# The fourth weight sum of a Strassen quad, moved from VectorE to an accumulating DMA

## The chip, the cores and the metric

The kernel runs on one core of a Trainium2 chip. The metric is the device time of one execution in microseconds (us); lower is better. The core has a matrix engine (TensorE, PE in the profile, with its weight loads as PEld), VectorE (DVE), ScalarE (ACT), GpSimd (POOL) and SyncE (SP), which mostly issues DMAs. All engines run their own instruction queues in order, and wait for each other through semaphores.

## The reference

One decoder layer on 256 tokens with model width 2048, all in float32: a first SwiGLU block (FFN, width 5632), then a mixer that joins sliding-window attention with a gated linear recurrence (HGRN2), a second SwiGLU block, gated per-layer input embeddings and a final RMSNorm.

```
def swiglu(h, w_gate, w_up, w_down):
    return (jax.nn.silu(h @ w_gate) * (h @ w_up)) @ w_down
...
    h = rmsnorm(x, ffn1_norm[l])
    x = x + 0.5 * swiglu(h, ffn1_w_gate[l], ffn1_w_up[l], ffn1_w_down[l])
    ...
    h = rmsnorm(x, ffn2_norm[l])
    x = x + 0.5 * swiglu(h, ffn2_w_gate[l], ffn2_w_up[l], ffn2_w_down[l])
```

The change lies in the two products `h @ w_gate` and `h @ w_up` of both FFNs.

## The kernel before, in words

**Weights.** All weights pass through the class `Weights` in one fixed order, as tiles of 128 x 1024 floats (512 KB). `load` issues a DMA from SP into a `raw` buffer (8 of them), three tiles ahead. `prep` makes two tiles of each: ACT casts `raw` to `whi` (line 117, `fp32r`), and DVE subtracts, `wlo = raw - whi` (line 118). There are 5 buffers of each. `next` is called by the code that multiplies, and keeps `prep` four tiles ahead of it. A product of float32 quality is made of three matmuls: activation high part by `whi`, activation low part by `whi`, activation high part by `wlo`.

**The FFN groups.** The width 5632 is cut into 11 column blocks of 512, worked in slices of two or three blocks, each followed by its part of the down-projection. In a block, `strassen_group` computes gate and up together. The contraction of 2048 is cut into four quarters, which go by the pattern S, P, S, P. In a P quarter the four weight tiles ("plain tiles") are used as they are, 12 matmuls each. In an S quarter ("quad") the four tiles are one 2 x 2 block matrix: b11 and b21 from gate, b22 and b12 from up. It is multiplied by seven products, Strassen's way, instead of eight; these are roles 0 to 6, six matmuls each. Roles 0, 1 and 2 use b11, b21 and b22 as loaded. The other roles use four sums that are made in place in the raw buffers:

```
b22 = b12 + b22        # used by role 4
b12 = b12 + b11        # used by role 5
b11 = b11 + b22        # used by role 3
b21 = b21 + b11        # used by role 6
```

So roles 3 to 6 each use a sum. All four are DVE instructions of line 101, the three of role 3's `prep` and the one of role 6's. The first FFN has ten such groups (its first column block is done plainly), the second eleven: 21 groups, 42 quads.

**Order.** The program is put in order by a scheduler, which gives each engine a static list: instructions go by priority once their inputs are expected. Loads and `prep` are in a block of high priority. Evictions of PSUM (lines 402 to 418), SiLU (468), the activations' scaling and transposes come between them. A raw buffer is free for the next load when its last reader has finished.

Of the kernel before, what the change touches and what calls it, by code (L numbers as in the profile page):

```python
# [15 lines left out]
ALU = mybir.AluOpType  # L16
# [15 lines left out]
class Weights:  # L32
# [61 lines left out]
    def prep(self, parts=1):  # L94
        nc = self.nc
        i = self.done
        self.done += 1
        while self.loaded < min(i + 1 + (LEAD if i > 12 else 0), len(self.order)):
            self.load(parts)
        key = self.order[i]  # L100
        add = lambda out, a, b: nc.vector.tensor_tensor(out, a, b, op=ALU.add)  # L101
        with self.tc.high_priority(offset=PRIO if i > 12 else 0):
            role = key[-1] if key[0] == "S" else 0
            raws = [self.raws.get(i - role + k) for k in range(4)]
            src = raws[(0, 1, 2, 0, 2, 3, 1)[role]]
            if role == 3:
                b11, b21, b22, b12 = raws
                add(b22, b12, b22)
                add(b12, b11, b12)
                add(b11, b11, b22)  # L110
            elif role == 6:
                add(raws[1], raws[1], raws[0])
            hi, lo = self.tile("whi", i, 5), self.tile("wlo", i, 5)
            n = 1024 // parts
            for p in range(parts):
                c = slice(p * n, (p + 1) * n)
                nc.scalar.copy(hi[:, c], src[:, c])  # L117
                nc.vector.tensor_tensor(lo[:, c], src[:, c], hi[:, c].bitcast(F32), op=ALU.subtract)  # L118
        if key[0] != "S":
            del self.raws[i]  # L120
        elif role == 6:
            for k in range(4):
                del self.raws[i - 6 + k]
        self.ready[i] = (hi, lo)
# [944 lines left out]
```

## Time and profile before

| | |
|---|---|
| median of 3 runs | 2217.03 us (2215.2 to 2217.91) |
| profiled execution | 2218.1 us; span 2216.0 us |
| granted TensorE clock | 0.995 |
| HBM read | 415.03 MB, 188 GB/s over the span |
| DMA queue of SP | 56.1% of 16 engines' span |
| DMA queue of ACT | 0.2% |
| DMAs issued by POOL | none |

The span runs from the first to the last instruction of the profiled execution. In a row of the time order stand the start, the time it took (several merged instructions have their count behind an x), the engine, the source line, the operation, and output and inputs by name; in brackets the engine's idle time before it and what ended it. A row of waits reads: engine, line, what it waited for, us in total, times, longest. `ps` are the PSUM banks of a Strassen group, `as` the activations of an S quarter, `ap` those of a P quarter.

### The profile page before, as it was taken

Reading aid. Unit: us, or ns where it says so; the run is one execution under the profiler, and the core shown is the slowest. Engines: PE = TensorE matmul, PEld = TensorE weight load, DVE = VectorE, ACT = ScalarE, POOL = GpSimd, SP = SyncE. Lnnn points to the kernel's source line nnn. Section 1 sums busy time; section 2 is a strip of 40 time slices with the busy share of each in tenths; the row PEclk is TensorE's granted clock in tenths of the full one; section 3 lists DMA queues with packets and bytes.
Section 4 is the critical chain, followed back from the end, with each engine's and each line's share of the span. In section 5 each row is a group of like instructions: output and inputs, shape, how many; then the busy total and the mean of one; then the engine's idle time right before and its main releaser. Section 6 shows DMA issues by size and latency. Waiting matters only on the chain.

```text
span 2216.0 us, 27978 instructions
## 1 busy us (share of the span) xinstructions
PE 2182.4 (98%) x10400; PEld 1795.3 (81%) x10400; DVE 1666.3 (75%) x1954; ACT 1168.4 (53%) x1482; POOL 12.7 (1%) x26
## 2 busy tenths in 40 slices
PE   8999999999999999999999999999999999999998
PEld 7778888888888888877888888787888888888887
DVE  6987979789796566776455555898897979789654
ACT  7644645455455444556444445565554545545554
POOL 0000000000000000000000000000000000000000
PEclk9999999999999999999999999999999999999999
DMA  8455556646466554544666665456555556646662
GB/s 305 166 204 171 201 180 227 210 171 228 155 245 185 182 166 151 158 146 148 191 190 191 189 190 180 152 193 217 185 217 176 191 189 219 212 177 221 201 195 87
DMA packets 118072, 418.97 MB, mean 189 GB/s; under 512 B 13744, under 2 KB 14128, under 8 KB 117936
## 3 DMA queue, kind: packets, MB, share of 16 engines
q1 hardware_dynamic: 117072, 415.83, 56.1%
q8 instruction: 82, 1.34, 0.2%
q10 hardware_dynamic: 864, 1.35, 0.2%
q14 instruction: 54, 0.44, 0.1%
HBM read 415.03 MB, written 2.10 MB: 188 GB/s over the span
## 4 chain that ended last, share of the span: by engine, by line
PE 94%; DVE 3%; DMA 1%; ACT 1%; issue 1%; POOL 0%; SPq 0%; ACTq 0%; POOLq 0%; DVEq 0%
PE ps L399 38%; PE pa L290 16%; PE pa L291 16%; PE pa L296 16%; PE pb L311 3%; PE pb L313 1%; DVE wlo L118 1%; PE tp L333 1%; PE lv L808 1%; DMA raw<-in_ffn_gate 1%; ACT whi L117 1%; DVE raw L101 1%; DMA x<-in_x 0%; PE tx L506 0%; PE sc L726 0%
## 5 line engine op out<-in xcount | busy, mean ns | idle before, releaser
L118 DVE TENSOR_TENSOR wlo<-raw,whi 128x1024 fp32r<-128x1024 f32 (+1 forms) x907 | 1079.4, 1219 | 446.1 <-ACT whi L117 440.9
L117 ACT CAST whi<-raw 128x1024 fp32r<-128x1024 f32 (+1 forms) x907 | 930.5, 1051 | 888.6 <-PE pa L291 468.1
L399 PE MATMUL ps<-whi,ap 128*128 128x512 f32 x1344 | 337.2, 389 | 3.2 <-ACT whi L117 3.2
L399 PE MATMUL ps<-whi,as 128*128 128x512 f32 x1176 | 318.8, 393 | 4.3 <-DVE ff L464 2.1
L399 PEld LDWEIGHTS ps<-whi,ap 128*128 128x128 f32 x1344 | 251.6, 188 | 57.5 <-ACT whi L117 4.5
L291 PE MATMUL pa<-whi,act 128*128 128x512 f32 x704 | 275.2, 392 | 3.9 <-DVE act L335 3.9
L290 PE MATMUL pa<-whi,act 128*128 128x512 f32 x704 | 277.3, 395 | 0.6 <-ACT act L334 0.6
L399 PEld LDWEIGHTS ps<-whi,as 128*128 128x128 f32 x1176 | 220.9, 189 | 55.8 <-ACT whi L117 3.0
L101 DVE TENSOR_TENSOR raw<-raw,raw 128x1024 f32<-128x1024 f32 x168 | 205.4, 1223 | 4.2
L290 PE MATMUL pa<-whi,hTmx 128*128 128x512 f32 x480 | 192.1, 400 | 0.0
L296 PE MATMUL pa<-wlo,act 128*128 128x512 f32 x704 | 190.2, 392 | 0.0
L291 PE MATMUL pa<-whi,hTmx 128*128 128x512 f32 x480 | 187.4, 391 | 0.0
L399 PE MATMUL ps<-wlo,ap 128*128 128x512 f32 x672 | 183.5, 390 | 2.5 <-DVE wlo L118 2.5
L399 PE MATMUL ps<-wlo,as 128*128 128x512 f32 x588 | 182.9, 392 | 0.0
L291 PEld LDWEIGHTS pa<-whi,act 128*128 128x128 f32 x704 | 132.9, 189 | 31.3 <-DVE act L335 4.6
L290 PEld LDWEIGHTS pa<-whi,act 128*128 128x128 f32 x704 | 132.8, 189 | 27.6 <-ACT act L334 0.9
L296 PEld LDWEIGHTS pa<-wlo,act 128*128 128x128 f32 x704 | 132.1, 189 | 27.3
L399 PEld LDWEIGHTS ps<-wlo,ap 128*128 128x128 f32 x672 | 126.1, 188 | 29.9 <-DVE wlo L118 3.8
L399 PEld LDWEIGHTS ps<-wlo,as 128*128 128x128 f32 x588 | 110.5, 189 | 24.4 <-DVE wlo L118 1.7
L296 PE MATMUL pa<-wlo,hTmx 128*128 128x512 f32 x480 | 128.4, 389 | 0.0
L290 PEld LDWEIGHTS pa<-whi,hTmx 128*128 128x128 f32 x480 | 90.1, 188 | 21.4 <-issue 2.5
L296 PEld LDWEIGHTS pa<-wlo,hTmx 128*128 128x128 f32 x480 | 90.1, 188 | 18.9
(238 smaller groups left out, 1994.2 us busy)
## 6 DMA issues: line engine op xcount, KB each, us to landing
raw<-in_ffn_up SPq DMA_DIRECT2D x176, 512.0 KB, 5.1
raw<-in_ffn_down SPq DMA_DIRECT2D x176, 512.0 KB, 4.7
raw<-in_ffn_gate SPq DMA_DIRECT2D x175, 512.0 KB, 4.7
raw<-in_w_ga SPq DMA_DIRECT2D x32, 512.0 KB, 3.5
raw<-in_w_gb SPq DMA_DIRECT2D x32, 512.0 KB, 3.5
raw<-in_w_out SPq DMA_DIRECT2D x32, 512.0 KB, 3.5
raw<-in_ple_gate SPq DMA_DIRECT2D x32, 512.0 KB, 3.5
raw<-in_w_i SPq DMA_DIRECT2D x16, 512.0 KB, 3.5
```

Of the source, the lines that this page charges most:

```text
L101: add = lambda out, a, b: nc.vector.tensor_tensor(out, a, b, op=ALU.add)
L117: nc.scalar.copy(hi[:, c], src[:, c])
L118: nc.vector.tensor_tensor(lo[:, c], src[:, c], hi[:, c].bitcast(F32), op=ALU.subtract)
L290: nc.tensor.matmul(ps[t], ks[:, 0, tok], hi[:, c], start=(j == 0 and c == 0), stop=False)
L291: nc.tensor.matmul(ps[t], ks[:, 1, tok], hi[:, c], start=False, stop=False)
L296: nc.tensor.matmul(ps[t], ks[:, 0, tok], lo[:, c], start=False, stop=(last and c == 1))
L311: nc.tensor.matmul(ps, hi[:, c], mov(c), start=(first and c == 0), stop=False)
L313: nc.tensor.matmul(ps[:, 0:S], lo[:, c], mov(c)[:, 0], start=False, stop=False)
L333: nc.tensor.transpose(pt[:, c, t * P:(t + 1) * P], srcs[t][:, i * P:(i + 1) * P], ident)
L399: nc.tensor.matmul(bank(i), stat, mov, start=done[i] == 1, stop=done[i] == todo)
L808: nc.tensor.matmul(ps[a * 64:a * 64 + 64, i], k[:, c], q[:, c], start=True, stop=True)
```

## The change

The add of role 6 is taken out. At the end of role 3's sums, three roles earlier in the program, GpSimd issues a DMA that reads b11 and adds it into b21, both in SBUF.

```
             if role == 3:
                 b11, b21, b22, b12 = raws
                 add(b22, b12, b22)
                 add(b12, b11, b12)
                 add(b11, b11, b22)
-            elif role == 6:
-                add(raws[1], raws[1], raws[0])
+                nc.gpsimd.dma_start(b21, b11, accum_op=ALU.add)
```

Role 6's cast and subtract read b21 as before.

More of the change, by code (lines that the diff above doesn't have):

```diff
@@ L110, in prep @@
                 add(b11, b11, b22)
-            elif role == 6:
-                add(raws[1], raws[1], raws[0])
+                nc.gpsimd.dma_start(b21, b11, accum_op=ALU.add)
             hi, lo = self.tile("whi", i, 5), self.tile("wlo", i, 5)
```

## Prediction

> **What bounds the kernel now.** I read the busy times first, then what TensorE (PE) waited for, then the order of time around one Strassen quad.
>
> ```profile
> PE 2182.4 (98%) x10400; PEld 1795.3 (81%) x10400; DVE 1666.3 (75%) x1954; ACT 1168.4 (53%) x1482; POOL 12.7 (1%) x26
> ...
> L118 DVE TENSOR_TENSOR wlo<-raw,whi 128x1024 fp32r<-128x1024 f32 (+1 forms) x907 | 1079.4, 1219 | 446.1 <-ACT whi L117 440.9
> L117 ACT CAST whi<-raw 128x1024 fp32r<-128x1024 f32 (+1 forms) x907 | 930.5, 1051 | 888.6 <-PE pa L291 468.1
> ...
> L101 DVE TENSOR_TENSOR raw<-raw,raw 128x1024 f32<-128x1024 f32 x168 | 205.4, 1223 | 4.2
> ```
>
> PE is busy 98% of the span, so only 2216.0 - 2182.4 = 33.6 us are idle: whatever is taken from VectorE (DVE), no more than that can come back. The four sums of a quad are line 101: 168 adds, so 42 quads, 1.22 us each. The change takes one of each four away: 42 x 1.22 = 51 us of DVE. Does PE wait for them? The waits of PE and ScalarE (ACT):
>
> ```profile
> PE ps L399 <- ACT whi L117: 3.8, 4, 2.6
> PE ps L399 <- DVE wlo L118: 2.5, 3, 1.3
> PE ps L399 <- DVE ff L464: 2.1, 1, 2.1
> PE pa L291 <- DVE act L335: 3.9, 2, 2.8
> ...
> ACT whi L117 <- DVE raw L101: 105.3, 31, 6.6
> ```
>
> ACT waits 105 us for the sums, but PE waits only 3.8 + 2.5 us in the Strassen groups for a whi or wlo tile. The sums are on ACT's path and almost nowhere on PE's. The order of time around one quad, the second of a slice, shows why:
>
> ```profile
> 346.72 5.00 DVE L101 TENSOR_TENSOR raw<-raw,raw 128x1024 f32<-128x1024 f32 x4
> 350.52 1.07 PE L399 MATMUL ps<-whi,as 128*128 128x512 f32 x4
> 350.57 3.91 ACT L117 CAST whi<-raw 128x1024 fp32r<-128x1024 f32 x4 [5.15 <-DVE raw L101]
> 351.66 8.04 DVE L118 TENSOR_TENSOR wlo<-raw,whi 128x1024 fp32r<-128x1024 f32 x7
> 352.92 1.46 SPq L92 DMA_DIRECT2D raw<-in_ffn_gate  x2
> 358.68 1.07 PE L399 MATMUL ps<-whi,as 128*128 128x512 f32 x4
> 359.58 0.61 PE L399 MATMUL ps<-wlo,as 128*128 128x512 f32 x2
> 359.78 1.06 ACT L117 CAST whi<-raw 128x1024 fp32r<-128x1024 f32 x1 [0.30 <-PE ps L399]
> ```
>
> The scheduler already issues the fourth sum directly behind the third. The four adds start at 346.72 and take 5.00; the last needs 1.26 of that, so the third ends at T = 350.46. At T + 0.11 ACT starts the casts of roles 3, 4, 5 and 6. PE begins role 0 at 350.52, role 6 at 358.68, and its wlo matmuls at 359.58.
>
> **What is removed.** After T, DVE's next work is the subtract of role 3, which needs ACT's cast: T + 0.11 + 1.05 = T + 1.16. Before, the fourth add occupied DVE until T + 1.26. So the 1.22 us mostly turn into a wait for that cast; DVE gains 0.1 us per quad where it has nothing else to put there, and up to 1.2 us where an eviction or a scaling is queued. I take the gain as 0. Its upper bound: the PE waits that the shown rows put down to ACT's whi and DVE's wlo, ff and act reach 2.6, 1.3, 2.1 and 2.8 us at the longest, and one add less shortens an episode by at most 1.2 us; four episodes make 5 us. One of them is FFN2's first group:
>
> ```profile
> 1399.97 1.19 PE L399 MATMUL ps<-whi,ap 128*128 128x512 f32 x4 [2.62 <-ACT whi L117]
> 1402.46 1.22 PE L399 MATMUL ps<-wlo,ap 128*128 128x512 f32 x2 [1.30 <-DVE wlo L118]
> ```
>
> **What is added.** Per quad one DMA, issued from GpSimd's queue (POOL), that reads b11 and b21 and writes b21. Its trigger waits for the third add. The one new wait is ACT's cast of role 6, which waits for the landing. Call L the time from T until that cast may start. Before, ACT came to it at T + 2.97 (three casts of about 0.98 behind T + 0.11). From then on ACT stands still until T + L; behind it in ACT's order are the casts of the next plain tiles and the evictions; DVE's subtract of role 6 and all behind it move to T + L + 1.1, where they stood at T + 4.6. DVE is thus later than before once L exceeds about 3.5.
>
> PE has a reserve. Cast (1.05), hand-over and subtract (1.22) take 2.4 us together, and PE wants wlo of role 6 at 359.58, so in this quad L may be 359.58 - 350.46 - 2.4 = 6.7 us before PE waits. The same for the third and fourth quad of the slice, and for the tightest quads elsewhere:
>
> ```profile
> 370.59 1.21 DVE L101 TENSOR_TENSOR raw<-raw,raw 128x1024 f32<-128x1024 f32 x1
> 379.99 0.61 PE L399 MATMUL ps<-wlo,as 128*128 128x512 f32 x2
> 389.12 5.01 DVE L101 TENSOR_TENSOR raw<-raw,raw 128x1024 f32<-128x1024 f32 x4
> 400.42 0.62 PE L399 MATMUL ps<-wlo,as 128*128 128x512 f32 x2
> ...
> 81.43 5.00 DVE L101 TENSOR_TENSOR raw<-raw,raw 128x1024 f32<-128x1024 f32 x4
> 91.54 0.62 PE L399 MATMUL ps<-wlo,as 128*128 128x512 f32 x2
> ...
> 1419.63 5.00 DVE L101 TENSOR_TENSOR raw<-raw,raw 128x1024 f32<-128x1024 f32 x4
> 1430.64 0.62 PE L399 MATMUL ps<-wlo,as 128*128 128x512 f32 x2
> 1502.18 5.00 DVE L101 TENSOR_TENSOR raw<-raw,raw 128x1024 f32<-128x1024 f32 x4
> 1512.68 0.62 PE L399 MATMUL ps<-wlo,as 128*128 128x512 f32 x2
> ```
>
> Third quad: T = 371.80, reserve 379.99 - 371.80 - 2.4 = 5.8. Fourth: T = 392.87, reserve 5.15. FFN1's second quad: T = 85.17, reserve 4.0. Second and last quad of FFN2's first slice: T = 1423.37 and 1505.92, reserves 4.9 and 4.4; the five quads from the one to the other lie between 4.4 and 5.2, mean 4.8.
>
> The first quad of a slice is different: PE takes the first plain tile after role 4, before roles 5 and 6.
>
> ```profile
> 326.10 5.01 DVE L101 TENSOR_TENSOR raw<-raw,raw 128x1024 f32<-128x1024 f32 x4
> 329.95 4.85 ACT L117 CAST whi<-raw 128x1024 fp32r<-128x1024 f32 x5 [5.15 <-DVE raw L101]
> 336.76 1.98 PE L399 MATMUL ps<-whi,ap 128*128 128x512 f32 x8
> ```
>
> T = 329.85. That plain tile is ACT's fifth cast, behind role 6. To be ready at 336.76 it must start by 335.6, so L may be 335.6 - 329.85 - 0.98 = 4.8.
>
> Eight slices (all but the first of each FFN) repeat this pattern of four. A stall of PE adds to the end one for one, since PE has no idle time left to absorb it. So the cost in us is: 8 x (L - 4.8) + 8 x (L - 5.15) + 8 x (L - 5.8) + 9 x (L - 6.7) + 5 x (L - 4.8) + (L - 4.0), each term only where positive (the nine include one quad of FFN1's first slice; in its other two, and in FFN2's first quad, PE already waits for other things).
>
> **The size of L.** No accumulating or SBUF-to-SBUF DMA is in the trace. The nearest rows are plain loads:
>
> ```profile
> DMA to landing us min/median/max: 3.3/4.1/9.7
> ...
> L92 SPq DMA_DIRECT2D raw<-in_ffn_gate x177: 327/328/732, 1.2 to 2006.0; - x177
> ...
> DMA packets 118072, 418.97 MB, mean 189 GB/s; under 512 B 13744, under 2 KB 14128, under 8 KB 117936
> ...
> raw<-in_w_ga SPq DMA_DIRECT2D x32, 512.0 KB, 3.5
> ...
> wide<-in_masks SPq DMA_DIRECT2D x1, 256.0 KB, 2.6
> ```
>
> Landings count from the issue; 256 KB land in 2.6 us, 512 KB in 3.5, so 0.9 us per 256 KB on a fixed 1.7. The sum must read two tiles of 512 KB; counting both, 1.7 + 4 x 0.9 = 5.3. With the wake-up (0.1) and an issue at least as dear as SP's (0.33 us) L = 5.8. Ends: 3.4 (the fastest plain landing plus the wake-up, as if the second read were free) and 9.7 (the slowest landing). I stay at 5.8, as twice the bytes of the nearest undisturbed row.
>
> The Trainium skill, "DMA: Bandwidth & Descriptors" (Anatomy of one DMA — SWDGE (gpsimd) path), fits a GpSimd DMA as 2.0 us + bytes / 436e3, which makes 3.2 us for 512 KB; the fastest landing of 3.3 agrees for a plain load. "Collectives: The Full Stack" (The bandwidth ceiling) says that a reducing DMA runs at about half the rate because it reads two sources on one ring, not because the add costs anything; by both pages an estimate is 2.0 + 2 x 1.2 = 4.4 us, and the sum would be about 0.4 us, no change. No trace here shows such a DMA.
>
> **The sum** at L = 5.8: 8 x 1.0 + 8 x 0.65 + 0 + 0 + 5 x 1.0 + 1.8 = 20 us, removed adds 0. Against the profiled execution (span 2216.0, 2218.1 in all, 1.1 above the median of the runs, 2217.0) this gives 2238, and 2237 on the median's scale. At L = 7 the formula gives 59 us, at 8 it gives 98.
>
> **Other queues.** POOL is passed by 42 triggers; what else it holds near them is small, such as the next row, which DVE releases 9 us after the third add of that quad (1393.78 + 1.22): cost 0.
>
> ```profile
> 1393.78 1.22 DVE L101 TENSOR_TENSOR raw<-raw,raw 128x1024 f32<-128x1024 f32 x1
> ...
> 1404.24 0.70 POOL L262 TENSOR_TENSOR rstdf<-rstdf,nhalf 128x2 f32<-128x2 f32 x1 [31.62 <-DVE rstdf L261]
> ```
>
> SP loads wait for raw buffers, and b11's now also waits for the DMA's read: T + 5.8 where it was T + 2.4. Loads of the next quad went out from 352.92; they can take the buffers of roles 4 and 5 first, one subtract (1.2 us) later each, and land by 354.1 + 4.1 = 358.2, before the cast that needs the first, 359.78. So 0; without that cover the 1.2 us would show once per quad. The DMA engines move 42 x 1 MB more reads, a tenth of the 419 MB; loads that cross it may land a microsecond later, which the same reserve hides.
>
> **The rivals.** (1) No change: the landing is shorter, because undisturbed it grows by only (3.3 - 2.6) = 0.7 per 256 KB: 1.9 + 2.8 + 0.1 = 4.8. The cost is 0.8 us: 2218. For it: little traffic right after T, since SP's next loads start 2.4 us later. Against: POOL's issue is then free. The two pages of the Trainium skill named above make this rival the likelier one. (2) Faster: the second read costs nothing, L = 3.4, below every reserve, and DVE's freed slots shorten the busy stretches: up to 5 us, 2212. It decides below L = 4.0. Against it: most stalls there start from ACT or from PSUM evictions as much as from the add. (3) Much slower: the add passes through the engines as three passes per byte (read, read, write), 1.7 + 6 x 0.9 + 0.4 = 7.5; the formula gives 78 us: 2295. Nothing in the trace speaks for or against.
>
> **How the numbers follow.** The forecast (L from 5.05 to 7.0) has 0.45, rival 1 0.28, rival 2 0.10, rival 3 with all beyond 7 0.17. A measurement can tell 0.2% (4.4 us) from no change: the cost passes 4.4 at L = 5.05. Hence faster 0.10, same 0.28, slower 0.62. The range runs from 2213, rival 2's side, to 2300; what is left out is below 0.2. Slower cases alone: 2222 to 2300.
>
> **What would show it.** Right: 126 adds in line 101; a cast of role 6 that waits 2 to 4 us for a raw<-raw DMA in most quads; PE waits on whi and wlo in the first and fourth quads of the slices, about 20 us more, none in the second. Wrong: PE's waits unchanged (L below 4.8); or all quads with waits of several us (L beyond 7); or ACT's order changed so that plain tiles are cast before role 6, which would lift the first quads' reserve and take 8 us off.

## The result, and the profile after

| | before | after |
|---|---|---|
| median of 4 runs each | 2217.47 us | 2240.55 us (2239.13 to 2242.07) |
| ratio after / before | | 1.0108 (95% interval 1.0096 to 1.012) |
| profiled execution, span | 2218.1, 2216.0 us | 2241.86, 2240.1 us |
| granted clock | 0.995 | 0.993 |

The kernel is 23 us slower; 2237 had been predicted. The busy times and groups of the profile page after:

```profile
PE 2190.5 (98%) x10400; PEld 1793.6 (80%) x10400; DVE 1617.3 (72%) x1912; ACT 1160.8 (52%) x1482; POOL 49.1 (2%) x68
...
q0 software_dynamic: 6048, 22.02, 5.2%
...
PE 58%; issue 18%; DVE 13%; DMA 4%; ACT 2%; POOL 0%; ACTq 0%; POOLq 0%; SPq 0%; DVEq 0%
...
L117 DVE TENSOR_TENSOR wlo<-raw,whi 128x1024 fp32r<-128x1024 f32 (+1 forms) x907 | 1082.8, 1219 | 519.5 <-ACT whi L116 508.8
...
L101 DVE TENSOR_TENSOR raw<-raw,raw 128x1024 f32<-128x1024 f32 x126 | 154.1, 1223 | 3.4
...
raw<-raw POOLq DMA_DIRECT2D x42, 512.0 KB, 4.5
```

The change did what it says. There are 126 adds where there were 168, DVE's busy time fell from 1666.3 to 1617.3 us, and GpSimd issues 42 DMAs that land 4.5 us after their issue. But in front of its subtracts DVE now idles 519.5 us instead of 446.1: 73 us more, where it was spared 49. The chain of work that ended last, before 94% PE, is now only 58% PE and runs through DVE (13%) and the new DMA (4%) as well; its 18% of "issue" is time for which the profile shows no wait. Of the 24.1 us between the two spans, 16.0 are more idle time of PE (2240.1 - 2190.5 = 49.6, before 33.6). The other 8.1 are longer busy time of PE on the same 10400 matmuls; the profile models where a matmul ends, so part of it can be short waits. Line numbers after the edit are one lower than before.

The waits after (engine, line, what it waited for: us in total, times, longest):

```profile
ACT whi L116 <- DVE raw L101: 156.5, 37, 6.7
...
ACT whi L116 <- DMA raw<-raw: 68.3, 33, 3.8
...
PE ps L398 <- ACT whi L116: 9.8, 11, 3.5
...
PE tp L332 <- DVE ff L474: 3.4, 4, 0.9
...
PE tp L332 <- DVE ff L472: 3.1, 4, 0.8
```

ACT waits 2.1 us at a time for the new DMA (68.3 / 33). PE's own waits for `whi` rose from 3.8 to 9.8 us. The last two rows, transposes (`tp`) that wait for the gated activations (`ff`) at the end of a slice, did not stand among PE's waits before.

Where the time went, from the first loads of three weights in the three traces (`w_i` is first loaded as FFN1 ends, `ple_gate` as FFN2 ends; `w_out`'s last load is the mixer's end). The rows are those of the raw tiles' loads, before and then after; the two times are the first and the last issue:

```profile
L92 SPq DMA_DIRECT2D raw<-in_w_out x32: 327/328/328, 1269.9 to 1355.3; - x32
L92 SPq DMA_DIRECT2D raw<-in_ple_gate x32: 327/328/328, 2076.2 to 2171.6; - x32
L92 SPq DMA_DIRECT2D raw<-in_w_i x16: 327/328/328, 703.4 to 954.9; - x16
```

```profile
L92 SPq DMA_DIRECT2D raw<-in_w_out x32: 327/328/328, 1281.8 to 1367.1; - x32
L92 SPq DMA_DIRECT2D raw<-in_ple_gate x32: 327/328/328, 2100.2 to 2195.6; - x32
L92 SPq DMA_DIRECT2D raw<-in_w_i x16: 327/328/328, 715.1 to 966.5; - x16
```

FFN1 takes 715.1 - 703.4 = 11.7 us more. The mixer takes (1367.1 - 715.1) - (1355.3 - 703.4) = 0.1, FFN2 (2100.2 - 1367.1) - (2076.2 - 1355.3) = 12.2, the rest 0.1. The loss lies in the FFNs alone. Matching the same-numbered matmuls of both traces cuts it further: FFN1's first slice +3.5, its other four +8.2; FFN2's first slice +2.2, its other four +10.

### The profile page after: what moved, and what is told of

The parts are those of the page before. It is cut to its first block, busy times and chain, and to the rows that moved or that the text cites. A ratio compares the mean times of both kernels' runs of the same rounds, so it can differ in the third digit from the quotient of the medians.

```text
span 2240.1 us, 28073 instructions
## 1 busy us (share of the span) xinstructions
PE 2190.5 (98%) x10400; PEld 1793.6 (80%) x10400; DVE 1617.3 (72%) x1912; ACT 1160.8 (52%) x1482; POOL 49.1 (2%) x68
## 3 DMA queue, kind: packets, MB, share of 16 engines
q0 software_dynamic: 6048, 22.02, 5.2%
## 4 chain that ended last, share of the span: by engine, by line
PE 58%; issue 18%; DVE 13%; DMA 4%; ACT 2%; POOL 0%; ACTq 0%; POOLq 0%; SPq 0%; DVEq 0%
PE ps L398 19%; PE pa L289 11%; PE pa L295 11%; PE pa L290 11%; DVE wlo L117 6%; DMA raw<-raw 4%; DVE raw L101 3%; PE pb L310 3%; DVE ff L401 2%; ACT whi L116 2%; PE pb L312 1%; PE lv L807 1%; PE tp L332 0%; DVE st L401 0%; DVE ff L474 0%
## 5 line engine op out<-in xcount | busy, mean ns | idle before, releaser
L117 DVE TENSOR_TENSOR wlo<-raw,whi 128x1024 fp32r<-128x1024 f32 (+1 forms) x907 | 1082.8, 1219 | 519.5 <-ACT whi L116 508.8
L101 DVE TENSOR_TENSOR raw<-raw,raw 128x1024 f32<-128x1024 f32 x126 | 154.1, 1223 | 3.4
```

## The experiments

The theory was that of the prediction: ACT's wait for the landing delays all that stands behind it on ACT and DVE, and that delay eats PE's reserve. Rivals were that the scheduler's new order of the instructions costs the time, or the DMA's traffic.

**The wait taken away.** The fourth sum is left out: role 6 multiplies b21 as it was loaded, so the removed add's work is gone and nothing takes its place.

```
-                nc.gpsimd.dma_start(b21, b11, accum_op=ALU.add)
```

> The DMA of the changed kernel is left out with nothing in its place: the fourth sum is not made at all, and role 6 uses b21 as loaded. By the order listing the engines' instruction order is nearly that of the changed kernel (28 rows of PE's order differ), not that of the kernel before (391 differ). Theory 1 (latency: ACT's cast of role 6 stands until the DMA has landed, DVE loses about 1.6 us per quad and hands the backlog to PE): without the wait the cast of role 6 starts at T + 3 instead of T + 5.2, the gaps of PE in the steady slices vanish, 2212 to 2218 us. Rival A (the new instruction order is what costs): the order stays, so 2235 to 2242. Rival B (traffic and descriptor writing): also about 2217, so this run does not tell it from theory 1.

2205.33 us against 2216.94 before: ratio 0.9946 (0.9933 to 0.996), 11.6 us faster. This instruction order is close to after's on PE (28 rows stand differently, against 391 to before), so the order is not what costs the time. The DMA with the wait for it is: 2240.55 - 2205.33 = 35 us, more than the whole loss, because without the add the kernel would be 11.6 us faster. That is below what was expected. `w_i` is first loaded at 697.1 and `ple_gate` at 2063.0, so 6.3 us come from FFN1 and 6.8 from FFN2; by matched matmuls 5.3 and 5.8 of them from the first slice of each, and 0.25 from each of the eight other slices. Part of it shows in PE's waits in the Strassen groups, which fell from 3.8 us for `whi` and 2.5 for `wlo` to these:

```profile
PE ps L397 <- ACT whi L115: 1.2, 1, 1.2
...
PE ps L397 <- DVE wlo L116: 0.6, 1, 0.6
```

The third quad of a slice in this kernel and in after, in order of time, shows the delay itself. Without the sum:

```profile
364.79 1.22 DVE L101 TENSOR_TENSOR raw<-raw,raw 128x1024 f32<-128x1024 f32 x1
...
365.11 1.07 PE L397 MATMUL ps<-whi,as 128*128 128x512 f32 x4
...
366.11 6.75 ACT L115 CAST whi<-raw 128x1024 fp32r<-128x1024 f32 x7 [0.57 <-DVE raw L101]
...
374.63 1.98 PE L397 MATMUL ps<-whi,ap 128*128 128x512 f32 x8
```

With the DMA:

```profile
375.84 1.07 PE L398 MATMUL ps<-whi,as 128*128 128x512 f32 x4
...
377.23 1.22 DVE L101 TENSOR_TENSOR raw<-raw,raw 128x1024 f32<-128x1024 f32 x1
...
378.56 2.95 ACT L116 CAST whi<-raw 128x1024 fp32r<-128x1024 f32 x3 [0.58 <-DVE raw L101]
...
378.98 0.86 POOL L111 DMA_DIRECT2D raw<-raw  x1 [21.96 <-DVE raw L101]
...
383.61 6.75 ACT L116 CAST whi<-raw 128x1024 fp32r<-128x1024 f32 x7 [2.11 <-DMA raw<-raw]
...
384.69 5.76 DVE L117 TENSOR_TENSOR wlo<-raw,whi 128x1024 fp32r<-128x1024 f32 x5 [1.55 <-ACT whi L116]
...
384.71 1.20 PE L398 MATMUL ps<-whi,as 128*128 128x512 f32 x4 [0.32 <-ACT whi L116]
...
386.55 1.99 PE L398 MATMUL ps<-whi,ap 128*128 128x512 f32 x8
```

Without the sum ACT casts seven tiles in one go. With the DMA it stops for 2.11 us behind role 5, DVE stops for 1.55 us, and PE waits for role 6's `whi`. From PE's role 0 to its first plain tile are 374.63 - 365.11 = 9.52 us without the sum and 386.55 - 375.84 = 10.71 with it: 1.2 us lost. The reason that matters more stands at the top. T, the end of the third add, comes 377.23 + 1.22 - 375.84 = 2.61 us after PE's role 0 here, and 364.79 + 1.22 - 365.11 = 0.90 there: the quad starts late already, because DVE brought the stop of the quad before with it (1.84 us at 362.16, for that quad's role 6). It is so in all eight steady slices, those behind the first of each FFN: in their third quad T is 2.1 to 3.5 us after role 0, and was 0.89 before the change.

**The traffic alone.** DVE's add stays, and the same DMA runs into a spare tile that nobody reads (one buffer of the mixer's temporaries, of three, makes room for it).

```
+                nc.gpsimd.dma_start(self.spare, b11, accum_op=ALU.add)
             elif role == 6:
                 add(raws[1], raws[1], raws[0])
```

> VectorE makes the fourth sum as before, and the same GpSimd DMA is issued at the same place, reading b11, but it accumulates into a spare tile that nobody reads (to make room, the pool of temporaries of the mixer has two buffers instead of three, so only the two FFNs are compared, by the start of the same matmuls). The traffic, GpSimd's work and the longer hold of b11's buffer stay; nobody waits for the sum. Theory 1 (latency): the FFNs lose under 2 us each against the kernel before, 2216 to 2221 us beside whatever the mixer does. Rival B (the traffic delays weight loads, GpSimd's descriptor writing slows VectorE, or b11's later release delays the next loads): most of the 12 us per FFN remains, 2230 to 2242.

2222.22 us, ratio 1.0027 (1.0016 to 1.0037). The DMAs are the same as after's:

```profile
spare<-raw POOLq DMA_DIRECT2D x42, 512.0 KB, 4.5
```

```profile
L94 SPq DMA_DIRECT2D raw<-in_w_out x32: 327/328/328, 1273.6 to 1359.0; - x32
L94 SPq DMA_DIRECT2D raw<-in_ple_gate x32: 327/328/328, 2080.6 to 2175.9; - x32
L94 SPq DMA_DIRECT2D raw<-in_w_i x16: 327/328/328, 704.1 to 955.1; - x16
```

FFN1 ends 704.1 - 703.4 = 0.7 us later, and FFN2 takes (2080.6 - 1359.0) - (2076.2 - 1355.3) = 0.7 more. The other 3.0 us arose in the mixer, where no such DMA runs and where this kernel has one buffer less. So the traffic, and the 0.86 us that GpSimd spends on each issue, cost some 1.4 us of the 35.

**Half of the sum by DMA, half by DVE.**

```
+                nc.gpsimd.dma_start(b21[:, 512:1024], b11[:, 512:1024], accum_op=ALU.add)
+                add(b21[:, 0:512], b21[:, 0:512], b11[:, 0:512])
```

> The DMA adds columns 512 to 1023 of b21 only, VectorE adds columns 0 to 511 (about 0.68 us by the shorter adds of line 402). The landing has half the bytes: the changed kernel's 4.5 us minus two times half a pass (8 packets of 159 ns are one pass of 1.27 us) gives 3.2 to 3.3 us, so the cast of role 6 may start at about T + 3.9 and waits 0.9 us instead of 2.2. Theory 1: the cost falls much more than by half, because the reserve covers 0.9 us: 2217 to 2224. Rival B (traffic): half of the 23 us, about 2229. Rival A (order): 284 rows of PE's order differ from the kernel before, so about 2235 or more.

2229.66 us, ratio 1.0055 (1.0043 to 1.0068): slower than the wait theory had it, and near what the traffic was given.

```profile
raw<-raw POOLq DMA_DIRECT2D x42, 256.0 KB, 3.3
...
ACT whi L117 <- DMA raw<-raw: 19.7, 18, 2.9
...
PE ps L399 <- DVE ff L402: 6.4, 9, 1.8
...
PE ps L399 <- DVE x L491: 4.4, 8, 1.3
```

The DMA did come sooner (3.3 us), and ACT's wait for it fell from 68.3 to 19.7 us. But PE's waits moved to DVE's evictions and residual sums (`ff`, `x`), and 284 PE rows stand differently from before. This one changes the order as well as the wait, and by itself decides nothing.

**The sum on GpSimd.** No DMA: GpSimd does the add itself.

```
+                nc.gpsimd.tensor_tensor(b21, b21, b11, op=ALU.add)
```

> GpSimd makes the fourth sum itself, as an add of 128 x 1024 between SBUF tiles, at the place of the DMA. No trace of this case shows such an add on GpSimd; from the rows of GpSimd (an add-like operation of 128x2 takes 0.7 us, a memset of 128x256 0.32) it may take 1.5 to 5 us. Theory 1: the cast of role 6 waits only if it takes more than 2.8 us; below that 2213 to 2219, at 4.5 us or more as the changed kernel, 2235 to 2242. Rival A (order; 28 rows differ from the changed kernel): 2235 to 2242 whatever its duration. A third possibility: VectorE's instructions get longer while GpSimd reads SBUF; then the mean of line 117 (VectorE's subtract) rises above 1219 ns.

2220.15 us, ratio 1.0017 (1.0008 to 1.0025). The add takes 2.41 us, so the cast of role 6 is not late: ACT comes to it at T + 2.96 as before. Still nothing is gained.

```profile
370.82 1.22 DVE L101 TENSOR_TENSOR raw<-raw,raw 128x1024 f32<-128x1024 f32 x1
...
372.26 2.41 POOL L111 TENSOR_TENSOR raw<-raw,raw 128x1024 f32<-128x1024 f32 x1 [19.78 <-DVE raw L101]
...
373.24 2.52 DVE L117 TENSOR_TENSOR wlo<-raw,whi 128x1024 fp32r<-128x1024 f32 x1
```

```profile
L117 DVE TENSOR_TENSOR wlo<-raw,whi 128x1024 fp32r<-128x1024 f32 (+1 forms) x907 | 1131.3, 1275 | 449.9 <-ACT whi L116 447.0
...
PE ps L398 <- DVE wlo L117: 10.3, 16, 1.7
```

The subtract that runs beside GpSimd's add takes 2.52 us instead of 1.22; it ends 1.09 us after the add does (375.76 against 374.67), as if it had begun only then. Over all 907 the mean is 1275 ns against 1219, (1275 - 1219) x 907 = 51 us: what was taken from DVE is taken back (its busy time is 1668.5 us, 1666.3 before). PE's waits stand on `wlo`. The Trainium skill says, in "Trainium Architecture — The Big Picture" (What this means for kernel authors), that on the engines' side of SBUF only the pair of ports shared by DVE and GpSimd contends, by an exclusive lock and not by sharing bandwidth; the 2.52 us agree.

**The wait kept, but given time.** Role 6 is used two plain tiles later, by PE and by `prep`; the DMA stays where it is.

```
-                        order.extend(("S", (g, c), (u, c), q, role) for role in range(7))
+                        order.extend(("S", (g, c), (u, c), q, role) for role in range(6))
...
-                        order.extend((v, (2 * q + k, c)) for k in range(2) for v in (g, u))
+                        order.extend((v, (2 * q, c)) for v in (g, u))
+                        order.append(("S", (g, c), (u, c), q - 1, 6))
+                        order.extend((v, (2 * q + 1, c)) for v in (g, u))
```

> The changed kernel, with role 6 moved in the order of weights, casts and products: it comes after the first two of the four plain tiles that follow each quad, instead of before them. The DMA is issued where it was. ACT's cast of role 6 now stands behind the casts of two plain tiles, which wait for PE at 2.7 us each, so it comes some 5 us later and the DMA has landed by then. Theory 1 (latency): the wait is covered and what the run without the sum saved stays saved, less the 1 to 2 us that the traffic costs: 2203 to 2212 us, clearly faster than the kernel before. Rival B (traffic, GpSimd, buffer release): the 35 us between the run without the sum and the changed kernel stay for the most part, 2230 or more. A new wait is possible: b11's and b21's raw buffers are held about 5 us longer, which would show as ACT's casts waiting for loads, 2215 to 2230.

2207.68 us against 2218.34: ratio 0.9954 (0.9941 to 0.9966), 10.7 us faster than before, where after is 23.1 slower than its own runs of before.

```profile
PE 2176.3 (99%) x10400; PEld 1796.5 (81%) x10400; DVE 1622.1 (74%) x1912; ACT 1169.6 (53%) x1482; POOL 49.2 (2%) x68
...
ACT whi L117 <- DMA raw<-raw: 4.6, 11, 1.0
...
PE ps L401 <- DVE ff L471: 3.7, 1, 3.7
```

The same 42 DMAs land in the same 4.5 us, and ACT waits 4.6 us for them instead of 68.3. The last row is PE's longest wait in the Strassen groups; those for `whi` and `wlo` come to 0.3 us each.

**The late place with DVE's add.** The same edit of the order, with the add of line 101 kept, in the program now at role 6's later `prep`. The scheduler still places it directly behind the third add, as in this quad:

```profile
344.32 5.00 DVE L101 TENSOR_TENSOR raw<-raw,raw 128x1024 f32<-128x1024 f32 x4
```

So this kernel differs from the last one in what makes the sum, and hardly in when it is started.

> The control for the last run: the same later place of role 6, with VectorE making the fourth sum at role 6's place as in the kernel before. If the new place alone were the gain, this runs as fast as the run with the DMA there. Theory 1: VectorE still has the 42 adds, so it stays within 5 us of the kernel before, 2212 to 2222, and the DMA version is 5 to 13 us faster than this one.

2213.04 us, ratio 0.9977 (0.9969 to 0.9986): 5.3 us faster than before. So of the 10.7 us the later place alone brings 5.3, and the DMA instead of the add another 5.4. Where the landing is covered, the change pays.

**A longer landing.** The DMA is cut into two of half the columns, issued one after the other.

```
+                for c in (slice(0, 512), slice(512, 1024)):
+                    nc.gpsimd.dma_start(b21[:, c], b11[:, c], accum_op=ALU.add)
```

> The changed kernel, with the DMA cut into two of 512 columns each, one behind the other on GpSimd's queue: the same bytes, one more issue of 0.86 us, so the sum is whole about 0.5 to 0.9 us later (L about 5.7 to 6.0 instead of 5.2). Theory 1: between the run without the sum (cast of role 6 at T + 3.0) and the changed kernel (T + 5.2) a microsecond of wait cost 35 / 2.2 = 16 us; at the later end of L the slope should be steeper, up to 42 per us: 2249 to 2275. Rival B (traffic): the bytes are the same, 2240, or a few us more for GpSimd's second issue.

2260.13 us, ratio 1.0188 (1.0174 to 1.0202), 41.8 us over its runs of before where after was 23.1 over its own: 18.7 us more.

```profile
ACT whi L117 <- DMA raw<-raw: 75.2, 31, 3.8
...
385.52 1.75 POOL L112 DMA_DIRECT2D raw<-raw  x2 [22.40 <-DVE raw L101]
...
391.56 1.20 PE L399 MATMUL ps<-whi,as 128*128 128x512 f32 x4 [0.65 <-ACT whi L117]
```

GpSimd is held for 1.75 us by the two issues. Role 6's cast starts at T + 5.70 in the median of the quads (half of them between 5.47 and 5.76), 0.5 us later than after's median of 5.19, and ACT's and PE's waits grow (PE's for role 6 in the third quad is 0.65 us, 0.32 in after). Half a microsecond, 42 times, makes 21 us; the kernel lost 18.7. That would fit almost every quad passing its delay on to the end in full beyond L = 5.2, where the prediction's formula has 8 + 5 + 8 + 1 = 22 quads that do; which quads did was not counted.

## Why the prediction was right, and where its steps were not

The time (2240.55 against 2237), the sign and the cause (role 6's cast held by the landing) were right. The terms of the sum were not. The prediction had a cost of 20 us and a gain of 0; measured were 35 and 11.6. Both came out too small, by 15 and by 11.6, and these two misses nearly cancel: that the time is so close is luck.

- **"I take the gain as 0."** The removed adds are worth 11.6 us. In the steady quads the step holds: without the sum, the cast still starts at T + 2.97 and role 6's subtract at T + 4.61, and a slice gains 0.25 us. In the two first slices it does not hold. The bound of 5 us counted one add less per episode of PE's waits, four in all; each first slice gained more than that bound by itself. A better guide stood in the windows of the trace of before: first a steady slice, then FFN2's first (the columns are us, then the busy time of PE, PEld, DVE, ACT and POOL, the granted clock, the DMA share and GB/s):

```profile
326.00:453.00 127.00, 127.00 (x568) 104.75 (x568) 108.31 (x109) 66.31 (x70) 0.00 (x0) 1.00 0.58 199
```

```profile
1390.00:1520.00 130.00, 125.90 (x544) 102.41 (x543) 121.73 (x122) 75.10 (x85) 0.70 (x1) 0.97 0.53 190
```

  In the steady slice PE is busy throughout, and fewer adds can bring next to nothing. In FFN2's first DVE is busy for 121.73 of 130 us and PE has idle time and a clock of 0.97: there DVE is the likely brake, and each add of 1.22 us that it is spared can count. Without the sum PE's idle time over the whole of that slice fell from 5.8 to 2.7 us, and its busy time on the same matmuls from 174.2 to 171.3; the bound had counted waits alone.

- **The size of L.** Predicted 5.8, measured 5.19 from the third add's end to the cast, in the median of the quads (half of them between 5.16 and 5.40); that is just inside the forecast's 5.05 to 7.0. The way to the issue was longer (0.53 us from the add's end, 378.45, to GpSimd's start, 378.98, for 0.1 of wake-up and 0.33 of issue), the landing shorter (4.5 us for 5.3). Half the bytes land in 3.3 us, so 512 KB of sum cost 1.2 us on top of that, where twice the plain step of 0.9 makes 1.8. That two tiles count double was right: the DMA's packets took twice as long as the loads' (the figures stand at the end). The landing of 4.5 us agrees with the 4.4 that the two pages of the Trainium skill in the prediction lead to. The "no change" that followed from it there fell all the same, with the next step. (The estimate of 0.4 us there took the landing for L. With the prediction's own 0.43 of wake-up and issue it becomes L = 4.8 and 1.2 us, still no change.)

- **The step that failed: the reserves.** At L = 5.16 the formula gives 8 x 0.36 + 8 x 0.01 + 5 x 0.36 + 1.16 = 6 us, at 5.19 not a microsecond more. The measured cost of the wait is 35. The formula read each quad's reserve from the trace of before and held T fixed to PE: every quad started as if the last had not waited. But DVE idles some 1.6 us more in each quad (the row at 384.69: 1.55; role 6's subtract starts at T + 6.27 in the median, T + 4.61 before), and does that work later, before the next quad's adds. Before, T in the third quad was 370.59 + 1.21 = 371.80 and PE's role 0 at this row:

```profile
370.92 1.07 PE L399 MATMUL ps<-whi,as 128*128 128x512 f32 x4
```

  That is 0.88 us; after it is 2.61, so the reserve of 5.8 was worth 5.8 - 1.73 = 4.1 when the wait came. The prediction had put the third quad at no cost; it lost 1.2 us, about the 5.16 - 4.1 that this leaves. It expected waits in the first and fourth quads: the fourth had none to speak of (its reserve, 5.15 before and 5.13 to 5.28 after, is just L), and in the first PE no longer took the plain tile between roles 4 and 6, so that its reserve was another and the 8 us expected there did not come. In all, PE's waits for `whi` and `wlo` in the Strassen groups came to 9.8 + 0.3 = 10.1 us, from 3.8 + 2.5 = 6.3: 4 us more, not the 20 that were to show there.

- **The end of the slice** was not in the sum at all. The same lateness of DVE holds up the gated activations that PE transposes next (after, at the end of the slice whose third quad is shown above):

```profile
421.23 1.28 DVE L472 TENSOR_TENSOR ff<-ff,ff 128x512 f32<-128x512 f32 x2
...
421.96 0.33 PE L332 MATMUL tp<-ident,ff 128*128 128x128 f32 x1 [0.78 <-DVE ff L472]
```

  Before, the weight load of the same transpose waited 0.15 us, and PE not at all:

```profile
414.80 0.14 PEld L333 LDWEIGHTS tp<-ident,ff 128*128 128x128 f32 x1 [0.15 <-DVE ff L473]
```

  The two rows of such waits in the result make 6.5 us in eight waits of 0.8.

- **Together.** After minus the kernel without the sum, by matched matmuls of the two profiled executions (spans 2240.1 and 2202.8): 20 us in the eight steady slices, 8.8 in FFN1's first, 8.0 in FFN2's first, near 0 elsewhere. The formula at its too long L gave 8 + 5.2 = 13.2, 1.8 and 5.0, so it was short in each. The eight steady slices alone cost what it gave for the whole; that is luck. The 8.0 us of FFN2's first slice go when the landing is covered: with the DMA and the later place of role 6 the slice takes 174 us, as without the sum. About half of the 8.0 is idle time of PE (7.0 us, 2.7 without the sum), the rest longer busy time on the same matmuls (175.0, 171.3). FFN1's first slice takes 3.0 us more in that run than without the sum; how its 8.8 divide stays open. There the granted clock fell as well, from 0.97 to 0.94 (before, then after):

```profile
0.00:165.00 165.00, 148.63 (x633) 118.11 (x634) 133.76 (x175) 103.86 (x144) 1.67 (x10) 0.97 0.64 227
```

```profile
0.00:168.00 168.00, 148.25 (x631) 118.49 (x631) 129.95 (x179) 103.06 (x144) 5.29 (x14) 0.94 0.68 234
```

- **Right:** the traffic and the loads cost next to nothing (0.7 us per FFN), and ACT's wait of 2 to 4 us per quad was 2.1 in the mean, in 33 of the 42 quads. Rivals 1 and 2 took L at 4.8 and 3.4; even at the measured 5.16 their sums would have stayed near no change. Rival 3 is out by its L alone.

## What to carry to other kernels

A wait that is moved onto an in-order engine is not paid from the reserve of its own step alone: what the engine did not do then, it does later, so compute the second and third step with the lateness of the first, and follow it to the end of the stage. When an operation is moved from a busy engine to a slow but free path, give its consumer a later place in the same edit: here the DMA cost 23 us with the consumer three casts behind, and gained 5.4 us with two tiles more between. Leaving the operation out altogether, for one run, tells what the removal is worth before its replacement is judged.

## What the runs showed of the hardware

- An accumulating DMA of 512 KB between two SBUF tiles, 128 x 1024 floats, lands 4.5 us after its issue; 256 KB in 3.3 us; its instruction holds GpSimd for 0.86 us. It starts 0.53 us after the end of the third add, where the DMA into the spare tile started 0.29 us after and GpSimd's own add 0.22 (372.04 to 372.26); why these differ stays open.
- Its 6048 packets took 5.2% of 16 engines' 2240.1 us. The 5376 among them of 4096 bytes took 341 ns in the median, where the weight loads' packets of that size took 159: adding a tile into another cost the DMA engines about twice a load of it.
- GpSimd's 42 DMA issues did not slow DVE: the subtracts' mean is 1219 ns before and after. GpSimd's own add did: the subtract beside it took 2.52 us instead of 1.22.
